# Attention logits: the second product contracts over 128 rows instead of 64

## The chip, the cores and the metric

One NeuronCore of one Trainium2 chip runs the whole layer. The metric is the time of one execution on the device in microseconds (us). Engines: TensorE (PE; its weight loads are listed as PEld), VectorE (DVE), ScalarE (ACT), GpSimd (POOL), and SyncE (SP), which issues most transfers.

## The reference

One decoder layer on 512 tokens of width 1024 in float32: a short convolution and a differential attention side by side, then cross-attention to a memory of 256 tokens, then a retrieval of experts (PEER). The part that matters here is the attention with 8 heads, each with two query/key pairs (c = 0, 1) of width 64:

```python
logits = jnp.einsum('bqhcd,bkhcd->bhcqk', qi, k).astype(jnp.float32) * scale
logits = logits + bias[None, :, None]
logits = jnp.where(rel[None, None, None] >= 0, logits, -1e30)
p = jax.nn.softmax(logits, axis=-1)
a = p[:, :, 0] - lam * p[:, :, 1]
return jnp.einsum('bhqk,bkhe->bqhe', a.astype(v.dtype), v)
```

## The kernel before

**Precision.** TensorE multiplies in a rounded float32 format (F32R). To keep precision each operand is split into an upper part (rounded) and a lower part (the rest), and a product is the sum of three: upper x upper, upper x lower, lower x upper. `split` makes the parts: the upper by ScalarE (L98), the lower by VectorE (L99). `project` (L120 in `product`) loads a weight of 1024x128 through SyncE, splits it and runs 8 x 3 products of 128 contracted rows and 512 columns into one PSUM bank `psmm`.

**Stages.** The memory's keys and values come first; then, for 8 heads, `diff_head` (attention) and `conv_channels` (convolution) by turns, which is the stage of this change; then gates and output projections, cross-attention, key scores, expert gates and the expert loop. The stage of `diff_head` lasts until some 413 us.

**One head.** `diff_head` projects queries, keys and values (three calls of `project`, weights 24 + h, 32 + h and 40 + h). A query or key half has 64 rows; c = 0 lies on partitions 0 to 63, c = 1 on 64 to 127 (`own`), and the remaining 64 partitions are `other`. The query tile `qs2[c]` holds the upper part of the query on `own` (L258) and its lower part on `other` (L259). The key tile `ks2[c]` holds the key's upper part on both halves (L262 on ScalarE; L264 copies it over on VectorE). So one product of 128 rows (L287) gives upper x upper plus lower x upper. The key's lower part lies in one tile `klo` for both c, each on its own half (L263); the second product (L288) adds upper x lower from 64 rows of both operands:

```python
nc.tensor.matmul(pl[:, :nm], qs2[c][:, qs], ks2[c][:, :nm], start=True, stop=False)
nc.tensor.matmul(pl[:, :nm], qs2[c][own[c], qs], klo[own[c], :nm], start=False, stop=True)
```

This pair runs for 4 query blocks and 2 values of c in 8 heads: 64 pairs, of 256 (blocks 0 and 1), 384 or 512 columns. VectorE adds the bias and takes the maximum (L290), ScalarE exponentiates (L295), VectorE combines the two (L297, L298), TensorE transposes (L301), the result is split (L98, L99, tiles `aw`) and multiplied with the values (L317, `pspv`, 256 columns).

**Buffers.** Tiles named `head` (queries, keys, `klo`, value parts; 7 per head) come from a pool of 12. The logits go through two PSUM banks `pslg`.

**Order.** The program is written head by head, but the order on each engine is set by the framework's scheduler, which simulates the program with its own cost model and places each instruction when its operands are ready there. Any change of an instruction or of a buffer can thus move others, anywhere behind it.

Of the kernel before, what the change touches and what calls it, by code (L numbers as in the profile page):

```python
# [14 lines left out]
F32 = mybir.dt.float32  # L15
# [4 lines left out]
AF = mybir.ActivationFunctionType  # L20
ALU = mybir.AluOpType
# [40 lines left out]
class Block:  # L62
# [184 lines left out]
    def diff_head(self, h, x):  # L247
        nc, a = self.nc, self.a
        tt = self.t("toep")
        tp = self.toep[h]  # L250
        nc.sync.dma_start(out=tt, in_=bass.AP(tensor=tp.tensor, offset=tp.offset + P - 1, ap=[[TAB - 1, P], [1, T]]))

        own, other = (slice(0, 64), slice(64, P)), (slice(64, P), slice(0, 64))
        head = lambda: self.t("head", dt=F32R)
        qs2, ks2, klo = [head() for _ in range(2)], [head() for _ in range(2)], head()
        pp = self.project(a["w_in"][24 + h], x)
        for c, q in enumerate(qs2):
            nc.scalar.activation(q[own[c]], pp[own[c]], AF.Copy, scale=0.125)  # L258
            nc.vector.scalar_tensor_tensor(out=q[other[c]], in0=pp[own[c]], scalar=0.125, in1=q[own[c]].bitcast(F32), op0=ALU.mult, op1=ALU.subtract)  # L259
        pp = self.project(a["w_in"][32 + h], x)  # L260
        for c, k in enumerate(ks2):
            nc.scalar.activation(k[own[c]], pp[own[c]], AF.Copy)  # L262
            nc.vector.tensor_tensor(out=klo[own[c]], in0=pp[own[c]], in1=k[own[c]].bitcast(F32), op=ALU.subtract)  # L263
            nc.vector.tensor_copy(k[other[c]], k[own[c]].bitcast(F32))  # L264
        pp = self.project(a["w_in"][40 + h], x)
        vt = self.t("vt")
        nc.scalar.copy(vt, pp)
        pt = self.ps("tr")
        for i in range(NT):
            nc.tensor.transpose(pt[:, i * P : (i + 1) * P], vt[:, i * P : (i + 1) * P], self.ident)  # L270
        vhi, vlo = self.t("head", dt=F32R), self.t("head", dt=F32R)
        self.split(vhi, vlo, pt)
        po = self.ps("pv")
        for pair in range(2):

            ahi = [self.t("aw", [P, 2, 2 * P], F32R) for _ in range(pair + 1)]
            alo = [self.t("aw", [P, 2, 2 * P], F32R) for _ in range(pair + 1)]
            for qi in range(2):
                qb = 2 * pair + qi
                n = (qb + 1) * P  # L280
                qs = slice(qb * P, (qb + 1) * P)
                st = self.t("st", [P, 8])
                e = []
                for c in range(2):
                    pl = self.ps("lg")
                    nm = max(n, 2 * P)
                    nc.tensor.matmul(pl[:, :nm], qs2[c][:, qs], ks2[c][:, :nm], start=True, stop=False)  # L287
                    nc.tensor.matmul(pl[:, :nm], qs2[c][own[c], qs], klo[own[c], :nm], start=False, stop=True)  # L288
                    s = self.t("lg")
                    nc.vector.tensor_tensor_reduce(out=s[:, :n], in0=pl[:, :n], in1=tt[:, (3 - qb) * P :], op0=ALU.add,  # L290
                                                   op1=ALU.max, scale=1.0, scalar=TINY, accum_out=st[:, c : c + 1])
                    e.append(s)
                nc.vector.tensor_scalar(out=st[:, 2:4], in0=st[:, 0:2], scalar1=-1.0, scalar2=None, op0=ALU.mult)
                for c in range(2):
                    nc.scalar.activation(e[c][:, :n], e[c][:, :n], AF.Exp, bias=st[:, 2 + c : 3 + c], accum_out=st[:, 4 + c : 5 + c])  # L295
                nc.vector.reciprocal(st[:, 6:8], st[:, 4:6])
                nc.vector.tensor_scalar(out=e[1][:, :n], in0=e[1][:, :n], scalar1=st[:, 7:8], scalar2=self.neglam, op0=ALU.mult, op1=ALU.mult)  # L297
                nc.vector.scalar_tensor_tensor(out=e[0][:, :n], in0=e[0][:, :n], scalar=st[:, 6:7], in1=e[1][:, :n], op0=ALU.mult, op1=ALU.add)  # L298
                pa = self.ps("tr")
                for k in range(qb + 1):  # L300
                    nc.tensor.transpose(pa[:, k * P : (k + 1) * P], e[0][:, k * P : (k + 1) * P], self.ident)  # L301
                cols = slice(qi * P, (qi + 1) * P)
                for b in range(pair + 1):
                    m = min(2, qb + 1 - 2 * b)
                    src = pa[:, 2 * b * P : (2 * b + m) * P].rearrange("p (k q) -> p k q", q=P)
                    self.split(ahi[b][:, :m, cols], alo[b][:, :m, cols], src)
                    if m == 1:

                        nc.gpsimd.memset(ahi[b][:, 1, cols].bitcast(F32), 0.0)
                        nc.gpsimd.memset(alo[b][:, 1, cols].bitcast(F32), 0.0)  # L310
            osl = po[:, pair * 2 * P : (pair + 1) * 2 * P]
            nk = 2 * pair + 2
            for k in range(nk):
                b, r = divmod(k, 2)
                ks = slice(k * P, (k + 1) * P)
                for p, (v, w) in enumerate(((vhi, ahi), (vhi, alo), (vlo, ahi))):
                    nc.tensor.matmul(osl, v[:, ks], w[b][:, r, :], start=(k == 0 and p == 0), stop=(k == nk - 1 and p == 2))  # L317
        raw, sq = self.t("rs"), self.t("rs")
        nc.scalar.copy(raw, po)
        nc.scalar.activation(sq, raw, AF.Square)  # L320
        r = self.t("rh", [P, NT])
        self.roots(r, sq, T, 1.0 / P, EPS_SUB, True)
        nc.vector.scalar_tensor_tensor(out=raw, in0=raw, scalar=self.g_sub, in1=self.spread(r, T), op0=ALU.mult, op1=ALU.mult)
        return self.split_new("B", raw)
# [617 lines left out]
```

## Time and profile before

| what | value |
|---|---|
| median of 3 runs | 2113.95 us (2107.61 to 2119.21) |
| the profiled execution: its own time | 2111.31 us |
| its span, first to last instruction | 2109.5 us |
| mean granted TensorE clock | 0.993 of full |
| TensorE busy | 2041.9 us, 97% of the span |
| VectorE, ScalarE, GpSimd busy | 71%, 48%, 16% |
| HBM traffic | 209 GB/s over the span |

How to read it: the profile belongs to one execution, whose time is 2.64 us below the median. Busy shares are averages over stages with different limits. The ends of products on TensorE are modelled, so a busy TensorE may still not be streaming all the time; what a product really takes is read from the distance to the next one, or from the chain of waits, where pieces are counted from end to end.

### The profile page before, as it was taken

The page shows a single profiled execution, that of the slowest core. Times are in us where ns is not written, and L with a number is a line of the kernel's source. Part 1 is how long each engine was busy: PE and PEld are TensorE (multiplying, and loading weights), DVE is VectorE, ACT ScalarE, POOL GpSimd, SP SyncE. Part 2 cuts the span into 40 slices and gives each one's busy share as a digit, 9 for nine tenths or more (in the row PEclk, how much of TensorE's full clock was granted, in tenths as well). Part 3 has the DMA queues.
Part 4 walks back from the last instruction along what each step waited for, and adds up shares of the span by engine and source line. Part 5 has one row for each costly group of instructions (what it writes and reads, how often), then busy time and mean ns, then how long its engine had stood idle before and what let it go on. Part 6 is the DMA issues. An engine that isn't in the chain of part 4 may idle for free.

```text
span 2109.5 us, 29182 instructions
## 1 busy us (share of the span) xinstructions
PE 2041.9 (97%) x10341; PEld 1769.4 (84%) x10341; DVE 1505.4 (71%) x3531; ACT 1002.1 (48%) x1716; POOL 347.3 (16%) x309
## 2 busy tenths in 40 slices
PE   8999999999999999999999999999999999999997
PEld 7877778788888788999999889988777877888985
DVE  6666566533454669999788776557878777987887
ACT  6544444422343443333489999943333333333332
POOL 1000000000000000011231110012222233654441
PEclk9999999999999999999999999999999999999999
DMA  8422222234332133355787776599999978899984
GB/s 306 131 84 72 76 80 73 78 100 141 105 114 80 38 119 120 95 176 184 241 308 260 278 256 234 203 317 332 325 344 331 342 269 309 319 354 356 360 284 150
DMA packets 162418, 440.11 MB, mean 209 GB/s; under 512 B 14808, under 2 KB 70120, under 8 KB 160224
## 3 DMA queue, kind: packets, MB, share of 16 engines
q1 hardware_dynamic: 124464, 300.98, 42.7%
q0 software_dynamic: 37808, 137.26, 18.1%
q8 instruction: 81, 1.33, 0.3%
q14 instruction: 65, 0.53, 0.1%
HBM read 394.13 MB, written 46.68 MB: 209 GB/s over the span
## 4 chain that ended last, share of the span: by engine, by line
PE 50%; issue 17%; DVE 12%; DMA 11%; POOL 4%; ACT 4%; SPq 0%; DVEq 0%; POOLq 0%; ACTq 0%
PE psmm L120 33%; PE pslg L120 5%; PE psmm L755 4%; DMA raw<-in_peer_v 4%; POOL res L823 3%; DMA res<-in_peer_v,e 3%; DVE lo L99 3%; PE pstr L755 2%; ACT slot L863 1%; DMA res<-in_peer_u,e 1%; ACT hi L98 1%; PE pspv L755 1%; PE pslg L288 1%; DMA res<-in_peer_u,kp 1%; DMA oh<-in_peer_v,e 1%
## 5 line engine op out<-in xcount | busy, mean ns | idle before, releaser
L98 ACT ACTIVATE hi<-raw 128x1024 fp32r<-128x1024 f32 x388 | 411.0, 1061 | 629.1 <-PE psmm L120 288.7
L99 DVE TENSOR_TENSOR lo<-raw,hi 128x1024 fp32r<-128x1024 f32 x388 | 473.5, 1221 | 271.0 <-ACT hi L98 263.7
L120 PE MATMUL psmm<-A,hi 128*128 128x512 f32 x1408 | 450.1, 396 | 1.9 <-DVE Yb L455 1.9
L120 PE MATMUL psmm<-n,hi 128*128 128x384 f32 x1472 | 393.9, 345 | 1.0 <-ACT sp L700 1.0
L120 PEld LDWEIGHTS psmm<-A,hi 128*128 128x128 f32 x1408 | 262.6, 188 | 59.4 <-issue 3.5
L120 PE MATMUL psmm<-A,lo 128*128 128x512 f32 x704 | 280.3, 398 | 0.0
L120 PEld LDWEIGHTS psmm<-n,hi 128*128 128x128 f32 x1472 | 269.0, 190 | 1.4 <-ACT sp L700 1.3
L120 PE MATMUL psmm<-n,lo 128*128 128x384 f32 x736 | 252.9, 344 | 4.8 <-DVE lo L99 4.5
L823 POOL DMA_INDIRECT res<-in_peer_u,e x85 | 94.2, 1108 | 449.5 <-DVE e L803 419.2
L120 PEld LDWEIGHTS psmm<-A,lo 128*128 128x128 f32 x704 | 132.6, 188 | 29.1 <-issue 2.4
L98 ACT ACTIVATE tr<-e 128x384 fp32r<-128x384 f32 x128 | 66.5, 520 | 176.6 <-DVE e L744 162.3
L120 PE MATMUL pslg<-n,hi 128*128 128x384 f32 x576 | 148.3, 338 | 0.0
L120 PEld LDWEIGHTS psmm<-n,lo 128*128 128x128 f32 x736 | 139.5, 190 | 8.0 <-DVE lo L99 7.9
L755 PE MATMUL psmm<-hi,tr 128*128 128x512 f32 x384 | 129.7, 400 | 15.1 <-ACT tr L98 8.1
L806 DVE CUSTOM_DVE_ANT_0 res<-res,hx 128x1024 f32<-128x1024 f32 x101 | 122.7, 1220 | 19.7 <-DMA res<-in_peer_u,e 12.1
L755 PE MATMUL psmm<-lo,tr 128*128 128x512 f32 x384 | 130.3, 393 | 1.5 <-DVE lo L99 1.4
L823 POOL DMA_INDIRECT res<-in_peer_v,e x74 | 105.8, 1429 | 120.2 <-DVE e L813 97.4
L823 POOL DMA_INDIRECT res<-in_peer_u,kp x16 | 20.5, 1278 | 617.3 <-DVE kp L803 577.3
L755 PE MATMUL psmm<-hi,e 128*128 128x512 f32 x384 | 119.3, 396 | 2.1 <-DVE e L803 1.2
L120 PEld LDWEIGHTS pslg<-n,hi 128*128 128x128 f32 x576 | 105.3, 188 | 3.1
L861 DVE TENSOR_SCALAR oh<-iota,e 128x128 f32<-128x128 f32 x384 | 107.0, 347 | 0.0
L817 DVE SCALAR_TENSOR_TENSOR acc<-res,e,acc 128x1024 f32<-128x1024 f32 x73 | 93.6, 1282 | 17.2 <-DMA res<-in_peer_v,e 17.0
(300 smaller groups left out, 3736.5 us busy)
## 6 DMA issues: line engine op xcount, KB each, us to landing
raw<-in_uT SPq DMA_DIRECT2D x128, 512.0 KB
raw<-in_peer_v SPq DMA_DIRECT2D x128, 512.0 KB
raw<-in_w_in SPq DMA_DIRECT2D x64, 512.0 KB
gates<-slot SPq DMA_DIRECT2D x16, 1536.0 KB
slot<-gates SPq DMA_DIRECT2D x16, 1536.0 KB
act<-sp SPq DMA_DIRECT2D x64, 192.0 KB
raw<-in_w_pq SPq DMA_DIRECT2D x16, 512.0 KB
raw<-in_w_ckv SPq DMA_DIRECT2D x12, 512.0 KB
```

The lines of the kernel that those rows point to most:

```text
L98: self.nc.scalar.activation(hi, src, AF.Copy)
L99: self.nc.vector.tensor_tensor(out=lo, in0=src, in1=hi.bitcast(F32), op=ALU.subtract)
L120: self.nc.tensor.matmul(out, ww[:, k, :], xx, start=(k == 0 and p == 0), stop=(k == KC - 1 and p == 2))
L288: nc.tensor.matmul(pl[:, :nm], qs2[c][own[c], qs], klo[own[c], :nm], start=False, stop=True)
L755: nc.tensor.matmul(accs[2 * i + half], l[:, ts], m[:, half * 512 : half * 512 + 512], start=(jj == 0 and p == 0), stop=(jj == NK - 1 and p ...
L806: nc.vector.tensor_tensor_reduce(out=t, in0=t, in1=hx, op0=ALU.mult, op1=ALU.add, scale=1.0, scalar=0.0, accum_out=wx[:, 0, s : s + 1])
L817: nc.vector.scalar_tensor_tensor(out=acc, in0=t, scalar=w, in1=acc, op0=ALU.mult, op1=ALU.add)
L823: nc.gpsimd.indirect_dma_start(out=t, out_offset=None, in_=a["peer_u"] if s < P else a["peer_v"], in_offset=bass.IndirectOffsetOnAxis(ap=i ...
L861: nc.vector.tensor_scalar(out=oh[:, 4 + w, :], in0=self.iota, scalar1=cols[:, 0, t - b * TB : t - b * TB + 1], scalar2=cols[:, 1, t - b * ...
L863: nc.scalar.copy(stage[:, :, q * 4 : q * 4 + 4].rearrange("p j w -> p w j"), pp.rearrange("p (w j) -> p w j", w=4))
```

## The change

The key's lower part gets a tile per c (`kl2[c]` in place of the shared `klo`). VectorE still writes it on `own`; a new ScalarE copy (L266 of the changed kernel) brings it to `other`. The second product then reads all 128 rows of both tiles, and computes upper x lower plus lower x lower.

```diff
-        qs2, ks2, klo = [head() for _ in range(2)], [head() for _ in range(2)], head()
+        qs2, ks2, kl2 = [head() for _ in range(2)], [head() for _ in range(2)], [head() for _ in range(2)]
...
-        for c, k in enumerate(ks2):
+        for c, (k, kl) in enumerate(zip(ks2, kl2)):
             nc.scalar.activation(k[own[c]], pp[own[c]], AF.Copy)
-            nc.vector.tensor_tensor(out=klo[own[c]], in0=pp[own[c]], in1=k[own[c]].bitcast(F32), op=ALU.subtract)
+            nc.vector.tensor_tensor(out=kl[own[c]], in0=pp[own[c]], in1=k[own[c]].bitcast(F32), op=ALU.subtract)
             nc.vector.tensor_copy(k[other[c]], k[own[c]].bitcast(F32))
+            nc.scalar.activation(kl[other[c]], kl[own[c]].bitcast(F32), AF.Copy)
...
-                    nc.tensor.matmul(pl[:, :nm], qs2[c][own[c], qs], klo[own[c], :nm], start=False, stop=True)
+                    nc.tensor.matmul(pl[:, :nm], qs2[c][:, qs], kl2[c][:, :nm], start=False, stop=True)
```

Two lines are added above the products, so L287 and L288 are L289 and L290 in the changed kernel, and L262 is L263. Counted without line and buffer numbers, the changed program has the same instructions on every engine but for 16 more on ScalarE. The scheduler's order moves. Two places show how.

TensorE, third head (h = 2), the second pair of logits products (c = 1) of the first query block. `pslg` is the logits' bank, `lg_1406` and `lg_1412` the previous head's weights under transposition. Before:

```order
L301 MATMUL pstr_1392<-ident,lg_1379 128x128 x2
L287 MATMUL pslg_1702<-head_1577,head_1575 128x256
L288 MATMUL pslg_1702<-head_1578,head_1575 128x256
L120 MATMUL psmm_1876<-A_881,lo_1880 128x512
L120 MATMUL psmm_1876<-A_887,hi_1879 128x512
```

And in the changed program:

```order
L303 MATMUL pstr_1398<-ident,lg_1385 128x128 x2
L289 MATMUL pslg_1711<-head_1583,head_1581 128x256
L120 MATMUL psmm_1852<-A_899,hi_1855 128x512
L120 MATMUL psmm_1852<-A_900,hi_1855 128x512
L120 MATMUL psmm_1852<-A_899,lo_1856 128x512
L120 MATMUL psmm_1852<-A_905,hi_1855 128x512
L120 MATMUL psmm_1852<-A_906,hi_1855 128x512
L120 MATMUL psmm_1852<-A_905,lo_1856 128x512
L120 MATMUL psmm_1852<-A_911,hi_1855 128x512
L120 MATMUL psmm_1852<-A_912,hi_1855 128x512
L303 MATMUL pstr_1425<-ident,lg_1412 128x128 x4
L290 MATMUL pslg_1711<-head_1585,head_1581 128x256
```

The two products of the pair stood next to each other; now eight projection products and four transposes stand between them.

ScalarE at the same head's keys (`head_1576` and `head_1577` are the two key tiles before; `head_1582` and `head_1583` in the change, `head_1584` and `head_1585` their lower parts). Before:

```order
L262 ACTIVATE head_1576<-psmm_1614 64x512
L98 ACTIVATE hi_1915<-raw_1913 128x1024
L267 COPY vt_1682<-psmm_1651 128x512
L98 ACTIVATE aw_1318<-pstr_1337 128x128
L98 ACTIVATE aw_1318<-pstr_1360 128x2x128
L262 ACTIVATE head_1577<-psmm_1614 64x512
```

And in the changed program:

```order
L263 ACTIVATE head_1582<-psmm_1621 64x512
L98 ACTIVATE aw_1324<-pstr_1343 128x128
L98 ACTIVATE aw_1324<-pstr_1366 128x2x128
L266 ACTIVATE head_1584<-head_1584 64x512
L263 ACTIVATE head_1583<-psmm_1621 64x512
L297 ACTIVATE lg_1412,st_1408<-lg_1412,st_1408 128x512
L297 ACTIVATE lg_1417,st_1408<-lg_1417,st_1408 128x512
L98 ACTIVATE hi_1924<-raw_1922 128x1024
L269 COPY vt_1691<-psmm_1660 128x512
L266 ACTIVATE head_1585<-head_1585 64x512
```

The two new copies (L266) stand in the queue, the second one behind a weight split (L98, 128x1024) and the copy of the values (L269), and the weight split has moved behind both key halves.

## Rows read from the trace of the kernel before

**Rows 1.** The page, parts 1 and 2: engines, and slices of the span in tenths.

```profile
PE 2041.9 (97%) x10341; PEld 1769.4 (84%) x10341; DVE 1505.4 (71%) x3531; ACT 1002.1 (48%) x1716; POOL 347.3 (16%) x309
...
PEclk9999999999999999999999999999999999999999
```

**Rows 2.** Table by stretches; behind the engines: granted clock, DMA share, GB/s.

```profile
80.00:415.00 335.00, 335.00 (x1578) 264.20 (x1577) 206.72 (x479) 153.40 (x326) 5.70 (x27) 1.00 0.26 77
600.00:900.00 300.00, 295.55 (x1481) 252.18 (x1480) 224.79 (x830) 123.40 (x206) 0.00 (x0) 0.99 0.30 93
900.00:1200.00 300.00, 288.86 (x1705) 281.19 (x1705) 252.80 (x708) 195.54 (x347) 62.35 (x52) 0.99 0.70 239
1200.00:2109.50 909.50, 867.20 (x4269) 754.00 (x4268) 698.06 (x1339) 424.91 (x665) 269.01 (x204) 0.99 0.85 299
```

**Rows 3.** Waits of the weight loader, 82 to 415 us: total, times, longest.

```profile
PEld pslg L288 <- issue: 12.9, 49, 0.4
PEld psmm L120 <- issue: 5.9, 27, 0.3
PEld pslg L287 <- issue: 0.6, 3, 0.2
PEld pslg L287 <- DVE lg L298: 0.2, 1, 0.2
PEld pslg L287 <- DVE lo L99: 0.2, 1, 0.2
```

**Rows 4.** Timeline of the loader from 92.8 us: start, duration, instruction, idle before.

```profile
92.84 0.19 PEld L287 LDWEIGHTS pslg<-head,head 128*128 128x128 f32 x1
93.27 0.18 PEld L288 LDWEIGHTS pslg<-head,head 64*128 64x128 f32 x1 [0.24 <-issue]
93.58 0.19 PEld L287 LDWEIGHTS pslg<-head,head 128*128 128x128 f32 x1
93.95 0.18 PEld L288 LDWEIGHTS pslg<-head,head 64*128 64x128 f32 x1 [0.18 <-issue]
94.32 0.19 PEld L120 LDWEIGHTS psmm<-A,hi 128*128 128x128 f32 x1 [0.19 <-issue]
94.43 0.19 PEld L120 LDWEIGHTS psmm<-A,lo 128*128 128x128 f32 x1
```

**Rows 5.** Chain of waits, 105 to 131 us: start, duration, work.

```profile
106.82 0.12 PE pslg L287
106.94 0.31 PE pslg L288
...
123.39 0.59 PE pspv L317 x5
123.98 0.18 PE pslg L287
124.15 0.12 PE pspv L317
124.27 0.37 PE pslg L288
124.64 0.43 PE pslg L287
125.07 0.43 PE pslg L288
...
127.67 2.53 PE psmm L120 x11
130.20 0.23 PE pslg L287
...
130.86 0.43 PE psmm L120
```

**Rows 6.** Groups by shape, TensorE and loader, 80 to 415 us: busy us, mean ns.

```profile
L288 PE MATMUL pslg<-head,head 64*128 64x256 f32 x32 | 12.2, 380 | 0.0
L288 PE MATMUL pslg<-head,head 64*128 64x512 f32 x16 | 8.0, 498 | 0.0
L288 PE MATMUL pslg<-head,head 64*128 64x384 f32 x16 | 7.0, 438 | 0.0
...
L287 PEld LDWEIGHTS pslg<-head,head 128*128 128x128 f32 x64 | 12.1, 189 | 3.0 <-issue 0.6 <-DVE lg L298 0.2 <-DVE lo L99 0.2
L288 PEld LDWEIGHTS pslg<-head,head 64*128 64x128 f32 x64 | 11.7, 183 | 14.8 <-issue 12.9
```

**Rows 7.** Groups by shape, ScalarE, 80 to 415 us.

```profile
L98 ACT ACTIVATE hi<-raw 128x1024 fp32r<-128x1024 f32 x45 | 47.7, 1060 | 70.7 <-PE psmm L120 59.3 <-issue 10.3 <-ACT lg L295 0.7
L262 ACT ACTIVATE head<-psmm 64x512 fp32r<-64x512 f32 x14 | 8.2, 589 | 4.2 <-DVE head L263 4.0
L267 ACT COPY vt<-psmm 128x512 f32<-128x512 f32 x8 | 4.6, 578 | 0.1
L98 ACT ACTIVATE Y<-cv 128x512 fp32r<-128x512 f32 x5 | 3.1, 621 | 0.0
```

**Rows 8.** VectorE's timeline at the second key half of heads 1 and 2; chain at the preceding heads' last pairs.

```profile
101.24 0.69 DVE L263 TENSOR_TENSOR head<-psmm,head 64x512 fp32r<-64x512 f32 x1
151.66 0.69 DVE L263 TENSOR_TENSOR head<-psmm,head 64x512 fp32r<-64x512 f32 x1
...
105.96 0.43 PE pslg L288
130.43 0.43 PE pslg L288
```

## The prediction

> **What bounds the kernel now.** I read the profile from the outside in. First the page: TensorE is busy for 97% of the span, its weight loads for 84%, every other engine for 71% or less, and the granted TensorE clock stands at 9 tenths or more in all 40 slices [rows 1]. So a price on TensorE counts if it stands where TensorE has no idle time. The two logits products run from 82 us to 393 us, and the table by stretches shows TensorE busy for 335.00 of the 335 us from 80 to 415, at clock 1.00 (the full 2.4 GHz level), while VectorE is busy for 62% of that time, ScalarE for 46%, the DMA engines for 26% [rows 2]. In this stage TensorE alone sets the pace.
>
> "Busy" does not say that it streams, though. The waits of its weight loader in this stage are led by the second logits product (L288): 12.9 us in 49 places, ended by nothing that the profile can name; next come the loads of the projections with 5.9 us [rows 3]. Waiting for data costs 0.4 us in two places. The loader's timeline shows what that is [rows 4]: a projection's load starts while the product before it still runs, and loads follow each other without a gap. The 64-row load of L288 starts late (0.24 and 0.18 us of idle), and so does the first 128-row load behind a 64-row one (0.19 us).
>
> The chain gives the price, because its pieces are counted from end to end. Behind a 128-row product the first logits product (L287) takes 0.12, 0.18 and 0.23 us for 256, 384 and 512 columns [rows 5]. These are the streaming prices: the value products, 256 columns wide, take 0.59/5 = 0.12 us each. The 64-row L288 takes 0.31, 0.37 and 0.43 us for the same widths, and whatever 128-row product follows it pays too: a projection product 0.43 us, where the normal one takes 2.53/11 = 0.23; a 512-column L287 behind an L288 also 0.43 [rows 5]. So it's not line 287 or 288, and not the two products into one bank: it is the step from 128 rows to 64 and the step back, about 0.19 us each way, which is the length of one load (0.183 us, [rows 6]). In one place a value product stands between L287 and L288, and the price stays with the L288.
>
> Here the Trainium skill has two rules. TensorEngine Tiling (Array Packing), Key Properties, says that changing the tiling mode, not only the tile, drains the engine; the trace agrees (0.31 us where 0.12 is normal). TensorE: Matmul & The Clock Gate, Part 3, says that a load overlaps running products only when the row groups differ; by that, loads of 128 rows would never be hidden, the change would win nothing, and the time would stay at 2111. The trace speaks against it: 128-row loads start under the product before them in [rows 4]. Measurement decides; the rule is kept as a rival below.
>
> **The change, part by part.** *Row count of the second product.* There are 64 pairs: 32 of 256 columns, 16 of 384, 16 of 512 [rows 6]. After the change each L288 reads 128 rows, has the same size of load as its neighbours, and should cost what L287 costs behind a 128-row product. Way in: 32 x (0.31 - 0.12) + 16 x (0.37 - 0.18) + 16 x (0.43 - 0.23) = 6.1 + 3.0 + 3.2 = 12.3 us. Way out: 64 x (0.43 - 0.23) = 12.8 us; every L288 is followed by a 128-row product. Together 25.1 us, all of it on an engine without idle time. The columns streamed do not change.
>
> *Sixteen added ScalarE copies* (new L266, 64x512, lower part of the keys to the other half; two per head). No row shows this form. Its nearest are the 64x512 read from PSUM at 0.589 us and the 128x512 copy from SBUF at 0.621 us [rows 7], so 0.6 us each, 9.6 us of ScalarE in all: 153.4 + 9.6 = 163 of about 310 us in the stage, 53%. As work this is covered by TensorE's products. As latency it may not be: the copy waits for VectorE's subtraction, and the second product now waits for the copy. Queued behind the copy on ScalarE stand the other key half, weight splits and exponentials. The order printed above shows that the second product of a head's first pairs has been moved some places back, up to 10 rows, so the program already leaves room. Lower bound 0: TensorE waits for data 0.4 us in the whole stage today [rows 3], although each key half has ScalarE and VectorE work before it. Upper bound: all 16 copies queue behind one weight split of 1.06 us with TensorE idle, 16 x (1.06 + 0.6) = 26.6 us. I take 1.3 us, close to the lower end, because the row of waits is the nearest case.
>
> *One more buffer.* A head takes 8 tiles named head instead of 7 from the same 12 buffers. A new wait is possible only where a head's keys are written before the preceding head's last pair is through. In the trace that is head 1 alone: its second key half is written at 101.24 us, head 0's last pair ends at 106.39 us; head 2's is written at 151.66 us, 20.8 us after head 1's last pair ends at 130.86 [rows 8]. The worst is 106.39 - 101.24 = 5.2 us once on VectorE, whose results are needed by TensorE only later; lower bound 0. I take 0.2 us.
>
> *Moved instructions.* The scheduler places the same TensorE, VectorE and DMA instructions slightly differently through the mixing stage and again in the last part of the expert loop; GpSimd's queue is unchanged, and SyncE's list has one weight load moved by one place. The bounds for that are what TensorE has idle where it could grow: 909.50 - 867.20 = 42.3 us in the last 909.5 us [rows 2]. I put 5 us either way and 0 in the sum.
>
> **The sum.** 2111.3 (time of the profiled execution; its span is 2109.5) - 25.1 + 1.3 + 0.2 = 2087.7, so about 2088 us, 1.1% faster. The median of the three runs is 2.6 us above the profiled execution; the runs spread over 11.6 us. Less than about 0.5% (10.6 us) can't be told from no change.
>
> After the stage TensorE stays the fullest engine: 295.6 of 300 us from 600 to 900, 288.9 from 900 to 1200, and 867.2 of 909.5 from 1200 on, where the DMA engines reach 0.85 [rows 2]. Work there starts in program order when its operands are there, so it should move forward by the same 25 us.
>
> **Rivals.** *Given back later* (chance 0.10). The last stage is held partly by transfers (DMA share 0.85) or the moved instructions there cost something. For: 42.3 us of idle TensorE in that stage shows waits. Against: those transfers are issued within the stage, so they move with it. A third to two thirds of the gain lost gives 2096 to 2104.
>
> *The change does not remove the step* (0.05). Loads stay exposed behind each other, for instance since every product then uses all row groups. For: the loads of 64 and 128 rows last the same, 0.183 and 0.189 us [rows 6], so the load itself becomes no cheaper. Against: the 0.12 us steps of [rows 5]. Time: 2111. The rule on row groups from TensorE: Matmul & The Clock Gate in the Trainium skill, named above, would make it this case.
>
> *TensorE waits for the copies* (slower, 0.04). Place: ScalarE's queue at each head's two key halves; the second product stands in order, so the projections behind it stop as well. A wait of 25.1/16 = 1.6 us per copy eats the gain; beyond (25.1 + 10.6)/16 = 2.2 us the kernel is measurably slower. A copy that stands behind a weight split (1.06) and a value copy of 0.58 us [rows 7] and takes 0.6 itself arrives 2.24 us late if TensorE is already there: 2111.3 - 25.1 + 35.8 = 2122. Against: ScalarE is idle for half of the stage, and TensorE does not reach the products that early.
>
> The forecast itself has 0.81.
>
> **Range and chances.** The forecast's own spread: waits of 0 to 8 us, 5 us from moved instructions, and some 4 us of run-to-run spread: 2079 to 2098. Taking in most of the given-back case extends it to 2102; the two remaining cases, 0.09, stay outside. Faster by over 0.5%: 0.81 and half of the given-back case, 0.86. Within 0.5%: the other half and the case without effect, 0.10. Slower: 0.04.
>
> **What would show it.** In the profile after: the second product reads 128 rows, its chain steps are 0.12, 0.18 and 0.23 us, the 12.9 us of the loader are gone, and the stretch of logits is about 25 us shorter at a TensorE that is still full. ScalarE shows 16 copies of about 0.6 us. Waits of the second product on ScalarE of more than 8 us in all would make the forecast wrong, as would steps of 0.3 us at 128 rows; a shorter stage with an unshortened kernel would be the given-back case.

## The result and the profile after

| | before | changed |
|---|---|---|
| median (6 runs each) | 2114.99 us | 2090.49 us |
| lowest and highest | 2107.61, 2119.21 | 2088.33, 2097.11 |
| ratio, 95% interval | | 0.9896 [0.9871, 0.9921] |
| profiled execution: time, span | 2111.31, 2109.5 | 2089.85, 2088.1 |

The change is 24.5 us (1.04%) faster between medians; between the two profiled executions it is 2111.31 - 2089.85 = 21.5 us. The page of the changed kernel, parts 1 and 2 (beside [rows 1]):

```profile
PE 2012.8 (96%) x10341; PEld 1765.4 (85%) x10341; DVE 1503.5 (72%) x3531; ACT 1010.7 (48%) x1732; POOL 354.0 (17%) x309
...
PEclk9999999999999999999999999999999999999998
```

TensorE has as many instructions as before, and is busy for 29.1 us less (2041.9 to 2012.8). ScalarE has 16 instructions and 8.6 us more. Where the time went is best read between two points that both programs pass after the same work: the first attention-stage projection (first L120 product on the tiles `A`) and the first output projection of the attention (first L120 product on the tiles `B`). The table by stretches, first the kernel before, then the changed one; columns as in [rows 2]:

```profile
63.80:511.50 447.70, 447.70 (x2081) 356.81 (x2080) 245.02 (x523) 185.85 (x372) 5.70 (x27) 1.00 0.29 87
```

```profile
62.80:485.40 422.60, 422.60 (x2081) 354.79 (x2080) 243.45 (x523) 194.50 (x388) 5.69 (x27) 1.00 0.30 92
```

Both stretches hold 2081 products, at a clock of 1.00 and with TensorE called busy throughout. One takes 447.70 us, the other 422.60: 25.10 us less. "Busy 100%" did hide the steps, as a product that waits for its weights is still counted as busy. The L288 at 93.28 us in the kernel before shows it: its load runs from 93.27 to 93.45 us [rows 4], and the product is counted as busy before its load has ended:

```profile
93.28 0.38 PE L288 MATMUL pslg<-head,head 64*128 64x256 f32 x1
```

The chain of the changed kernel (start, duration, work; compare [rows 5]) shows the price of the second product (L290, L288 before) at all three widths, and no price behind it:

```profile
107.58 0.12 PE pslg L289
107.70 0.12 PE pslg L290
107.82 0.12 PE pslg L289
107.94 0.12 PE pslg L290
108.06 2.99 PE psmm L120 x13
...
117.88 0.18 PE pslg L289
118.05 0.18 PE pslg L290
118.23 0.23 PE pslg L289
118.46 0.23 PE pslg L290
```

These are not chosen places. Counted from end to end over the whole stretch between the two points, the kernel before has 64 steps from 128 rows to 64 and 64 steps back, and every one pays: 0.31 to 0.32, 0.37 and 0.43 us on average for 256, 384 and 512 columns, both ways, where a product without a step takes 0.12, 0.18 and 0.23. The excess adds up to 12.4 us on the way in and 12.7 on the way out, 25.1 us. The changed kernel has no such step.

The groups of the weight loader, 70 to 400 us (busy us, mean ns, idle before; compare [rows 6]), and of ScalarE with the new copy (compare [rows 7]):

```profile
L290 PEld LDWEIGHTS pslg<-head,head 128*128 128x128 f32 x64 | 12.1, 189 | 1.3
L289 PEld LDWEIGHTS pslg<-head,head 128*128 128x128 f32 x64 | 12.1, 188 | 1.7
...
L266 ACT ACTIVATE head<-head 64x512 fp32r<-64x512 f32 x16 | 10.1, 631 | 9.0 <-DVE head L264 8.8
```

The load of the second product has not become shorter (183 before, 189 ns now). It is only no longer waited for: the 12.9 us of [rows 3] are gone, and the waits of TensorE and of its loader between 70 and 400 us are an empty list. The loader's timeline shows the four loads of two pairs running into each other, as only the projections' did in [rows 4]:

```profile
90.60 0.19 PEld L289 LDWEIGHTS pslg<-head,head 128*128 128x128 f32 x1
90.82 0.19 PEld L290 LDWEIGHTS pslg<-head,head 128*128 128x128 f32 x1
90.94 0.19 PEld L289 LDWEIGHTS pslg<-head,head 128*128 128x128 f32 x1
91.06 0.19 PEld L290 LDWEIGHTS pslg<-head,head 128*128 128x128 f32 x1
```

### The profile page after: what moved, and what is told of

It is laid out like the page before. It is cut to its first block, busy times and chain, and to the rows that moved or that the text cites. A ratio compares the mean times of both kernels' runs of the same rounds, so it can differ in the third digit from the quotient of the medians.

```text
span 2088.1 us, 29190 instructions
## 1 busy us (share of the span) xinstructions
PE 2012.8 (96%) x10341; PEld 1765.4 (85%) x10341; DVE 1503.5 (72%) x3531; ACT 1010.7 (48%) x1732; POOL 354.0 (17%) x309
## 4 chain that ended last, share of the span: by engine, by line
PE 47%; DMA 15%; DVE 14%; ACT 12%; issue 9%; POOL 3%; SPq 0%; ACTq 0%; DVEq 0%; POOLq 0%
PE psmm L120 33%; DMA raw<-in_peer_v 5%; ACT slot L865 5%; DMA res<-in_peer_v,e 4%; DVE lo L99 3%; PE pslg L120 3%; PE psmm L757 3%; ACT sq L857 3%; ACT hi L98 2%; PE pstr L757 2%; DMA res<-in_peer_u,e 1%; DMA act<-sp 1%; ACT oh L858 1%; DMA oh<-in_peer_v,e 1%; DVE acc L819 1%
## 5 line engine op out<-in xcount | busy, mean ns | idle before, releaser
L98 ACT ACTIVATE hi<-raw 128x1024 fp32r<-128x1024 f32 x388 | 409.8, 1059 | 605.0 <-PE psmm L120 302.1
L120 PE MATMUL psmm<-A,hi 128*128 128x512 f32 x1408 | 445.9, 393 | 1.9 <-DVE Yb L457 1.9
L120 PE MATMUL psmm<-n,hi 128*128 128x384 f32 x1472 | 394.2, 345 | 1.9 <-ACT sp L702 1.9
L120 PEld LDWEIGHTS psmm<-A,hi 128*128 128x128 f32 x1408 | 262.7, 188 | 54.7 <-DVE Yb L457 2.1
L120 PE MATMUL psmm<-A,lo 128*128 128x512 f32 x704 | 277.9, 395 | 0.0
L120 PEld LDWEIGHTS psmm<-n,hi 128*128 128x128 f32 x1472 | 269.3, 190 | 2.4 <-ACT sp L702 2.3
L120 PE MATMUL psmm<-n,lo 128*128 128x384 f32 x736 | 253.0, 344 | 5.0 <-DVE lo L99 4.8
L825 POOL DMA_INDIRECT res<-in_peer_u,e x85 | 94.7, 1114 | 450.5 <-DVE e L805 422.6
L120 PEld LDWEIGHTS psmm<-A,lo 128*128 128x128 f32 x704 | 132.4, 188 | 25.2
L98 ACT ACTIVATE tr<-e 128x384 fp32r<-128x384 f32 x128 | 66.5, 520 | 179.2 <-DVE e L746 173.7
L757 PE MATMUL psmm<-hi,tr 128*128 128x512 f32 x384 | 128.4, 400 | 21.6 <-ACT hi L98 12.4
L120 PE MATMUL pslg<-n,hi 128*128 128x384 f32 x576 | 148.3, 338 | 0.0
L120 PEld LDWEIGHTS psmm<-n,lo 128*128 128x128 f32 x736 | 139.5, 190 | 7.9 <-DVE lo L99 7.8
L120 PEld LDWEIGHTS pslg<-n,hi 128*128 128x128 f32 x576 | 105.3, 188 | 3.1
L757 PEld LDWEIGHTS psmm<-hi,tr 128*128 128x128 f32 x384 | 71.3, 190 | 40.0 <-ACT hi L98 13.9
```

What stands on the lines that cost most here:

```text
L98: self.nc.scalar.activation(hi, src, AF.Copy)
L120: self.nc.tensor.matmul(out, ww[:, k, :], xx, start=(k == 0 and p == 0), stop=(k == KC - 1 and p == 2))
L757: nc.tensor.matmul(accs[2 * i + half], l[:, ts], m[:, half * 512 : half * 512 + 512], start=(jj == 0 and p == 0), stop=(jj == NK - 1 and p ...
L825: nc.gpsimd.indirect_dma_start(out=t, out_offset=None, in_=a["peer_u"] if s < P else a["peer_v"], in_offset=bass.IndirectOffsetOnAxis(ap=i ...
```

## The experiments

Theory: every step between a product of 128 rows and one of 64, either way, exposes one weight load, about 0.19 us; there were 128 such steps, and nothing else of the change matters. TensorE's order between the two points moves in most of these programs as well; where that matters, the text says in how many of the 2077 places another product stands (line and buffer numbers and the row count left aside). For every run the table gives the time between the two points named above (in its profiled execution), the rest of that execution's span, and the measured ratio to the kernel before.

| run | 128-row second product | between the points | rest | ratio, 95% interval |
|---|---|---|---|---|
| before | none | 447.7 | 1661.8 | 1 |
| changed kernel | all | 422.6 | 1665.5 | 0.9896 [0.9871, 0.9921] |
| rows alone (e1) | all | 422.4 | 1656.0 | 0.9858 [0.9837, 0.9879] |
| copies alone (e2) | none | 455.3 | 1663.6 | 1.0048 [1.0025, 1.0071] |
| c = 0 on 64 rows (e3) | half | 434.8 | 1658.7 | 0.9929 [0.9909, 0.9949] |
| c = 1 on 64 rows (e3) | half | 444.2 | 1661.3 | 0.9976 [0.9959, 0.9992] |
| 64 rows twice (e5) | none | 458.8 | 1672.1 | 1.0078 [1.0050, 1.0106] |
| other stationary tile (e6) | all | 422.6 | 1659.2 | 0.9904 [0.9880, 0.9928] |
| copies, pool of 11 (e7) | none | 447.5 | 1659.1 | 0.9996 [0.9981, 1.0011] |
| zero half (e8) | all | 422.5 | 1658.2 | 0.9886 [0.9861, 0.9912] |
| the change again (e9) | all | 422.6 | 1656.3 | 0.9864 [0.9842, 0.9885] |
| rows alone again (e10) | all | 422.3 | 1657.5 | 0.9876 [0.9854, 0.9898] |

Every kernel with 128 rows in all second products needs 422.3 to 422.6 us between the points. The rest, the 1656 to 1672 us that the change should not touch, differs from one execution to the next by up to 16 us, and by 9.2 us between two executions of one kernel, the changed one (1665.5 and 1656.3).

**Rows alone (e1).**

```diff
-                    nc.tensor.matmul(pl[:, :nm], qs2[c][own[c], qs], klo[own[c], :nm], start=False, stop=True)
+                    nc.tensor.matmul(pl[:, :nm], qs2[c][:, qs], klo[:, :nm], start=False, stop=True)
```

> The kernel before, and only the second logits product reads all 128 rows of the query tile and of the shared key tile (it adds lower x lower of the other key half, which the reference does not have). No ScalarE copies, no eighth tile. Theory (each step between 128 and 64 rows exposes one weight load, about 0.19 us, 128 steps): the whole 25 us come back without the copies, about 2089 us beside 2114, ratio 0.987 to 0.990; steps of the second product 0.12, 0.18, 0.23 us in the chain. Rival (the gain comes from the second tile and the moved order): within 5 us of the kernel before. Rival (the copies cost something on the path): faster than the change by more than 3 us.

Measured: 2086.28 us, ratio 0.9858, and 422.4 us between the points. The whole gain comes without the copies and without a second tile, so the added buffer did not make it. This run does not rule out the order, which moved here too (805 of 2077 places against the kernel before); the zero half (e8) does, with 118 places moved and 422.5 us. Against the changed kernel it is 4.2 us faster, which is what the second rival named (more than 3 us); e9 and e10 take that up.

**Copies alone (e2).** The changed kernel with

```diff
-                    nc.tensor.matmul(pl[:, :nm], qs2[c][:, qs], kl2[c][:, :nm], start=False, stop=True)
+                    nc.tensor.matmul(pl[:, :nm], qs2[c][own[c], qs], kl2[c][own[c], :nm], start=False, stop=True)
```

> The changed kernel with its two key tiles and its 16 ScalarE copies, but the second logits product reads 64 rows again. Theory: no gain, 2114 to 2117 us, ratio 1.000 to 1.002; steps of the second product 0.31, 0.37, 0.43 us and 0.43 us for a projection product behind it. Rival (order and buffers made the gain): 2090 us. Rival (the copies hold TensorE up): over 2119 us.

Measured: 2124.01 us against 2115.62, ratio 1.0048: no gain, but 8.4 us slower, more than the theory's 3. By its time it is the second rival (over 2119 us); the cause is another one, as this trace and e7 show. Between the points it needs 7.6 us more than the kernel before. Its chain shows where, at the end of the stage, at the roots of the last head (L144 sums, L171 spreads; pieces as in the chain above):

```profile
433.77 0.80 PE pstr L144 x8
...
434.70 1.23 DVE lo L99
...
436.54 1.14 PE pstr L171 x8
...
439.13 1.28 ACT L347
...
440.42 0.61 ACT T L347
...
441.07 79.13 PE psmm L120 x336
```

From 434.57, the end of the sums, to 441.07 TensorE runs nothing but the spread of 1.14 us: a hole of 6.50 - 1.14 = 5.4 us, in which it waits for a VectorE split, small operations, and a ScalarE line (L347) of 1.28 us. In this program the scheduler has put L171 directly behind L144 and left nothing between them; in the kernel before 26 projection products stand there and in the changed kernel 29. The clock answers to the hole; table by stretches of the same run:

```profile
400.00:434.00 34.00, 34.00 (x173) 28.56 (x171) 15.36 (x25) 13.12 (x23) 0.00 (x0) 1.00 0.28 90
434.00:438.00 4.00, 1.68 (x13) 1.43 (x13) 2.03 (x6) 1.05 (x3) 0.00 (x0) 0.99 0.22 69
438.00:444.00 6.00, 2.93 (x7) 2.35 (x8) 1.83 (x3) 3.00 (x4) 0.00 (x0) 0.50 0.37 129
444.00:446.00 2.00, 2.00 (x9) 1.60 (x8) 0.00 (x0) 0.00 (x0) 0.00 (x0) 0.82 0.00 0
446.00:460.00 14.00, 14.00 (x63) 11.40 (x62) 3.44 (x4) 3.20 (x4) 0.00 (x0) 1.00 0.24 76
```

The granted clock is full (2.4 GHz) until the hole, stands at 0.50 (the 1.2 GHz level) from 438 us on, and is full again behind some 444.7 us (0.82 over the stretch from 444 to 446 us), although TensorE is busy from 441.07 us on. For 3.7 us products therefore run at half speed, which loses about 1.8 us. The chain agrees: the 336 products behind it take 79.13 us, 0.2355 each, where the kernel before has 84.78 us for 369, 0.2298 (its chain stands below): 336 x 0.0057 = 1.9 us. Hole 5.4, clock 1.9 and a spread that is 0.25 us longer than usual (1.14 against 0.89) make 7.6 us, all that the stretch is longer. The kernel before at the same place:

```profile
425.50 0.89 PE pstr L171 x8
426.39 84.78 PE psmm L120 x369
```

That leaves nothing for the copies, but by subtraction only, as the order differs too (921 places). The run with a pool of 11 (e7) takes the hole away.

**Half of the pairs (e3, two runs).** The changed kernel with

```diff
+                    rows = own[0] if c == 0 else slice(0, P)
-                    nc.tensor.matmul(pl[:, :nm], qs2[c][:, qs], kl2[c][:, :nm], start=False, stop=True)
+                    nc.tensor.matmul(pl[:, :nm], qs2[c][rows, qs], kl2[c][rows, :nm], start=False, stop=True)
```

> The changed kernel, but the second product of c = 0 (partitions 0 to 63) reads 64 rows; c = 1 stays at 128. Theory: half of the 128 steps are back, so 12.5 us over the change, 2102 to 2104 us, ratio to before 0.994. Rival (the price hangs on which half of the partitions is read): all of the 25 us back here or none, and the opposite with c = 1.

and the mirror of it for c = 1:

> The same for c = 1 (partitions 64 to 127): 64 rows for c = 1, 128 rows for c = 0. Theory: the same as with c = 0, 2102 to 2104 us, ratio 0.994. Rival (partition half): differs from the run with c = 0 by 10 us or more.

Measured: c = 0 at 2102.19 us, as the theory said (434.8 us between the points, 12.2 over the changed kernel: half of 25). c = 1 at 2110.86, 8.7 us more, close to what the rival wanted. It is not the partition half, though: this program has the same hole as the copies alone, 419.87 + 0.80 to 427.87 us in its chain, of which 1.83 is the spread.

```profile
419.87 0.80 PE pstr L144 x8
...
422.64 1.83 PE pstr L171 x8
...
427.87 87.34 PE psmm L120 x369
```

The hole is 7.20 - 1.83 = 5.4 us, the spread 0.94 us longer than 0.89, and the 369 products behind it take 87.34 - 84.78 = 2.6 us more: 8.9 of the 9.4 us between the two runs. (The granted clock of this run is 0.68 from 420 to 428 us, 0.57 from 428 to 434 and 1.00 from there to 446.) Without it 444.2 - 8.9 = 435.3, as for c = 0.

**64 rows twice (e5).** The changed kernel with

```diff
-                    nc.tensor.matmul(pl[:, :nm], qs2[c][:, qs], kl2[c][:, :nm], start=False, stop=True)
+                    nc.tensor.matmul(pl[:, :nm], qs2[c][own[c], qs], kl2[c][own[c], :nm], start=False, stop=False)
+                    nc.tensor.matmul(pl[:, :nm], qs2[c][own[c], qs], kl2[c][own[c], :nm], start=False, stop=True)
```

> The changed kernel, but in place of the second product of 128 rows stand two products of 64 rows on the same half, one behind the other (upper x lower is added twice). There are 64 more products, and still 128 steps between row counts. Their streaming alone is 32 x 0.12 + 16 x 0.18 + 16 x 0.23 = 10.4 us. Theory (the step between row counts costs, not the 64 rows): a 64-row product behind a 64-row product takes 0.12, 0.18, 0.23 us, total 2114 + 10 = 2124 us. Rival (every load of 64 rows is exposed): it takes 0.31, 0.37, 0.43 us, total 2114 + 10 + 12 = 2136 us.

The chain (L290 is the first product of 64 rows, L291 the second):

```profile
112.80 0.12 PE pslg L289
112.91 0.31 PE pslg L290
113.22 0.11 PE pslg L291
113.34 0.32 PE pslg L289
...
124.87 0.36 PE pslg L290
125.23 1.50 PE pspv L320 x11
126.73 0.37 PE pslg L291
127.10 0.43 PE pslg L289
127.53 0.43 PE pslg L290
127.96 0.23 PE pslg L291
```

A 64-row product behind a 64-row product takes 0.11 to 0.12 us at 256 columns and 0.23 at 512, the streaming price; the 128-row product behind it pays 0.32. Where the value products stand between the two, the second 64-row product pays again (0.37), and so does the first value product (11 take 1.50 us, where 1.30 is usual). The step is what costs, and 64 rows by themselves do not. (Both products of 64 rows load the same weights here; that equal weights are not what hides a load is shown in e6, for 128 rows.) Of the 64 added products 61 stand directly behind a 64-row one and take 0.12, 0.18 and 0.23 us on average; 3 do not, so there are 67 steps each way where the expectation counted 64. Between the points it is 11.1 us more than before, for 10.4 of added streaming and about 1.2 of added steps.

The total is no such clear sign: 2131.05 us, 17 more than before, lies between the 2124 of the theory and the 2136 of the rival. The rest of this execution is the longest of all, 1672.1 us, 10.3 more than in the kernel before. The same instructions stand there, and TensorE's order is that of the kernel before up to the 7165th product of 7841 behind the second point; 6.4 of the 10.3 us have arisen by the 7000th. So it is probably spread, which is not shown.

The Trainium skill states in TensorEngine Tiling (Array Packing), Key Properties, that a change of the tiling mode, not only of the tile, drains the engine. The trace agrees for the change of mode (0.31 us against 0.11); no run here changes the tile within a mode.

Does a step cost a load, or a drain of fixed length? All loads at the logits have 128 columns and take 0.18 to 0.19 us, so the experiments can't tell. One other place of the kernel before bears on it: at 17 us stand two products of 32 rows and 320 columns (L216) whose load has 8 columns and takes 82 ns. The pieces of the chain there, and the load's group:

```profile
17.30 0.36 PE pslg L216
17.66 0.27 PE pslg L216
17.93 0.32 PE psmm L120
...
L216 PEld LDWEIGHTS pslg<-rs,vt 32*8 32x8 f32 x4 | 0.2, 82 | 0.3
```

The way in costs 0.36 - 0.27 = 0.09 us, about the short load; the way out, to a load of 128 columns, costs 0.32 - 0.12 = 0.20 us. So the price goes with the length of the load that comes next, as the theory says. It is one form (the same twice in the kernel before, at 17 and 21 us), in plain float32 (not F32R) and with another row count, so it is a strong hint and no experiment.

**Another stationary tile (e6).** In the changed kernel the two products of a pair load the same query tile, so the load might be hidden for that reason only.

```diff
-                    nc.tensor.matmul(pl[:, :nm], qs2[c][:, qs], kl2[c][:, :nm], start=False, stop=True)
+                    nc.tensor.matmul(pl[:, :nm], qs2[1 - c][:, qs], kl2[c][:, :nm], start=False, stop=True)
```

> The changed kernel, but the second product takes the query tile of the other c as its stationary operand (so the logits are not the reference's). In the changed kernel both products of a pair load the same tile; here never. Theory: steps of the second product stay at 0.12, 0.18, 0.23 us, about 2090 us. Rival (the load is hidden only because the same tile is loaded twice): 0.31, 0.37, 0.43 us and 2102 us or more.

Measured: 2091.94 us, 422.6 us between the points, and steps as in the changed kernel:

```profile
103.34 0.23 PE pslg L289
103.57 0.23 PE pslg L290
103.80 0.23 PE psmm L120
104.03 0.12 PE pslg L289
104.15 0.12 PE pslg L290
```

TensorE's order between the points is that of the changed kernel in every place, so nothing else on TensorE differs. That rival falls.

**Copies alone, without the hole (e7).** As e2, and the pool of the tiles `head` smaller by one, which gives the scheduler another order at the end of the stage:

```diff
-        "head": ("h", 12), "toep": ("h", 2), "vt": ("h", 1), "lg": ("h", 4), "aw": ("h", 7), "rs": ("h", 2), "cv": ("h", 2),
+        "head": ("h", 11), "toep": ("h", 2), "vt": ("h", 1), "lg": ("h", 4), "aw": ("h", 7), "rs": ("h", 2), "cv": ("h", 2),
```

> The kernel with the copies and 64 rows once more, but with 11 buffers for the tiles named head instead of 12. With 12 the scheduler puts the transposing products of the last head's roots directly behind its sums, with no projection between them; with 11 it keeps 19 + 10 projection products there, as in the changed kernel. Theory (the 8 us that the copies seemed to cost are a hole of 5.5 us and a lower clock behind it, at the end of the stage, made by the order): no hole, 2113 to 2118 us, ratio 0.999 to 1.002. Rival (the copies themselves cost 8 us): 2122 us or more, ratio 1.004.

Measured: 2111.43 us against 2114.28, ratio 0.9996 [0.9981, 1.0011]; 447.5 us between the points where the kernel before has 447.7. Its chain there has no hole:

```profile
417.18 0.79 PE pstr L144 x8
417.97 6.73 PE psmm L120 x29
424.70 0.89 PE pstr L171 x8
425.59 94.54 PE psmm L120 x412
```

So 16 copies of 0.63 us cost nothing on the path as work of ScalarE, with one buffer less besides, and the 8.4 us of e2 belong to the order. As something to wait for they are not tested here, because in e2 and e7 the second product reads only the half that VectorE writes. That shows in the changed kernel itself: every copy ends at least 2.8 us before the first product that reads its half starts (closest at the third head, 144.24 and 147.08 us), and between the points it needs 422.6 us, where the same products without copies need 422.3 to 422.4 (e1, e10).

**A version without copies (e8).** Two lasting tiles hold the lower parts; their other halves are set to zero once, so that the second product adds exactly what it added before. The edit is shown against the kernel before; the lines of VectorE and of the second product are those of the changed kernel, and the ScalarE copy is left out.

```diff
-        "head": ("h", 12), "toep": ("h", 2), "vt": ("h", 1), "lg": ("h", 4), "aw": ("h", 7), "rs": ("h", 2), "cv": ("h", 2),
+        "head": ("h", 10), "kzo": ("h", 2), "toep": ("h", 2), "vt": ("h", 1), "lg": ("h", 4), "aw": ("h", 7), "rs": ("h", 2), "cv": ("h", 2),
...
-        qs2, ks2, klo = [head() for _ in range(2)], [head() for _ in range(2)], head()
+        qs2, ks2, kl2 = [head() for _ in range(2)], [head() for _ in range(2)], self.kz
...
+            self.kz = [self.t("kzo", dt=F32R) for _ in range(2)]
+            for c, kl in enumerate(self.kz):
+                nc.gpsimd.memset(kl[slice(64, P) if c == 0 else slice(0, 64)].bitcast(F32), 0.0)
```

> A version without copies and exact in the terms of the kernel before: two lasting tiles hold the keys' lower parts, and their other halves are set to zero once; the second product reads 128 rows; the pool has 10 + 2 buffers. Theory (only the row count counts): as with the rows alone, 2085 to 2090 us, ratio 0.986 to 0.988, stage between first attention projection and first output projection 333 us. Rival (lasting tiles make the next head's keys wait for the logits of this one): stage over 336 us.

Measured: 2087.84 us, ratio 0.9886, 422.5 us between the points. It saves ScalarE 10 us of work that nobody waits for, and is as fast as the change, no faster. Of all programs with 128 rows its order on TensorE is the nearest to the kernel before (118 of 2077 places differ, in the changed kernel 723), so the moved order is not what makes the gain.

**The change and the rows alone, side by side (e9, e10).** No edit.

> The changed kernel itself, on the same chip as the next run. The rows alone were 4 us faster than the change in another job, at equal length of the stage. Theory (run-to-run spread of the expert loop): the two differ by less than 3 us here. Rival (copies or their order cost 4 us): the change is 4 us or more slower again.

> The kernel before with 128 rows in the second product and nothing else, beside the change on one chip. Theory: within 3 us of the change. Rival: 4 us or more faster.

Measured: 2084.97 and 2086.48 us, 1.5 us apart, the change ahead this time. So the 4 us between the first two comparisons were spread. Here the change is 29.3 us faster than before (2114.28), in the first comparison 24.5. The 25.1 us of the stage lie inside the 95% interval both times (17 to 27 us in the first, 24 to 33 here).

## Why the prediction was right

- *The bound.* TensorE alone sets the pace of the stage, though its busy share can't shrink on the page: 100% before and after.
- *The step between row counts*, 25.1 us in the sum: measured 25.10 us between two points with 2081 products on both sides. Its two halves, the way in and the way out, are both shown in e5, where each is seen at a place of its own, and e3 gives half of the steps for half of the price. All 128 steps, counted one by one, add up to 12.4 and 12.7 us; the prediction had 12.3 and 12.8.
- *The copies*, 1.3 us in the sum, 0 to 26.6 as bounds: 0.63 us each as estimated from the rows, and on the path at most 0.3 us (e7: 447.5 against 447.7 as work; 422.6 against 422.3 to 422.4 in e1 and e10 as a wait; TensorE's list of waits in the stage is empty). The term of 1.3 us was too large. The order leaves the room that the prediction read from it: no copy ends less than 2.8 us before it is needed.
- *One more buffer*, 0.2 us: nothing that shows. Even 11 buffers are enough (e7).
- *Moved instructions*, 0 with 5 us either way: in the change itself nothing beyond the spread of the rest. But the bound was too narrow as a statement on such edits, and its place was wrong. It was drawn from idle time in the last 909.5 us; the real risk lay at the end of the attention stage, where a neighbouring order costs 7.6 to 9 us (e2, c = 1 of e3). The changed kernel's order has 29 products there, so it has no hole; the prediction did not ask about that place, and that it came out well there is luck.
- *Given back later*, as a rival: the profiled executions suggest it (25.1 in the stage, 21.5 in the end). The rest of the span was 1665.5 us in that execution and 1656.3 in e9 with the same program, so it is spread.
- *The change does not remove the step*, and with it the rule on row groups from TensorE: Matmul & The Clock Gate (Part 3) in the Trainium skill: 128-row loads behind 128-row products are hidden at all three widths, with the same stationary tile and with another (e6: 0.12 and 0.23 us). For this kernel the measurement decides against that rule.
- *Sum and total.* 2088 us were predicted, 2090.49 measured. The sum was made against an execution of 2111.31; against the median of 2114.99 it would have been 2091. That the total agrees so closely is partly luck, as the same two kernels were 24.5 us apart in one comparison and 29.3 in the other; what the runs show firmly is the 25.1 us between the two points.

## What to carry to other kernels

A product that contracts over fewer rows than its neighbours can cost two weight loads, one on the way in and one on the way out (0.19 to 0.20 us each here), that no other product pays; look for it where the loader waits for "issue" and the chain's pieces are longer than the streaming price, for the busy share does not show it. If full height is to be had with work on an idle engine, or with zeros, that is cheaper; if not, put products of the same height together (a 64-row product behind one on the same half ran at the streaming price in e5; regrouping this kernel's pairs was not tried). Before a small edit of a scheduled program is judged, read the order at the ends of stages: an unrelated hole there was worth a third of this gain.

## What the runs showed that was not expected

A program that differs from the changed kernel in the height of the second products alone (those of c = 1, or all 64) can get another order behind the last head, with nothing between the sums and the spread of the last head's roots. TensorE then stands for 5.4 us, and the granted clock falls to 0.50, the 1.2 GHz level, and stays there for some microseconds after TensorE is busy again (3.7 us in e2): 1.9 to 2.6 us on top of the hole. What in the scheduler's cost model tips the order wasn't tried.
